# An opening stage written out channel by channel over three row ranges: a hybrid mLSTM / sliding-window-attention encoder

## The chip, the cores and the metric

One Trainium2 chip, one core. The metric is the device time of one execution in microseconds (us): the median of the runs, 1853.66 for the kernel before.

## The reference

Two sequences pass through the same two-layer trunk: a prompt of 256 rows and a sample of 512 rows, 1024 channels wide. Each layer computes six modulation vectors from a condition vector, mixes along the sequence (layer 0: an mLSTM with gates; layer 1: attention in a window), and applies a convolutional feed-forward network. What the change touches is the beginning of layer 0:

```python
mod = jax.nn.silu(c) @ adaln_w[l] + adaln_b[l]
sh1, sc1, g1, sh2, sc2, g2 = [t[:, None, :] for t in jnp.split(mod, 6, axis=-1)]
h = rmsnorm(x, norm_g[l, 0]) * (1 + sc1) + sh1
...
proj = h @ w_in          # q, k, v, o and the gates
```

`rmsnorm` multiplies each row by the inverse root of its mean square, and then each channel by a gain. So h is x times a *factor* of the row, times a *gain* of the channel (from `sc1` and the norm's weights), plus a *shift* of the channel (`sh1`).

## The kernel before, in words

All rows lie side by side as 768 columns: columns 0 to 255 are the prompt, 256 to 767 the sample. Channels are on the 128 partitions, in KC = 8 chunks ("channels" below means such a chunk). Work on columns goes over three ranges of 256: `RANGES = ((256, 512, 0), (512, 768, 0), PROMPT)`: two of the sample, then the prompt.

Each product is made of three: activations and weights are split into a rounded high part and the rest (`hh`, `hl`, tiles `zh`, `zl`; `whi`, `wlo`), and a matmul of them is high by high, high by low and low by high. The split of a weights tile of 128x1024 is a copy on ScalarE (`fp_copy_split`, L259) and a subtraction on VectorE (L260). Three `whi` and three `wlo` buffers exist, five `raw` buffers for loads, and eight `nt` buffers for temporaries. Matmuls issue from the helper `mm` (L253).

The opening, in `first` (L1510) and the beginning of `mlstm` (L633):

- `adaln(0, 0)` (L388) multiplies the condition by 16 tiles of 512 KB of `adaln_w` on TensorE as they land; its end (L418 to L439) evicts the result to `sb`, transposes it (L422), and makes `mod` (shift) and `gain`.
- `Norm` (L89) squares the eight channels of a range on ScalarE (L110), adds some squares on GpSimd (L114), sums the rest over partitions on TensorE against `inv` (L145), takes the power -0.5 on GpSimd (L152) and spreads the factor over a PSUM bank `pr` by a matmul. `scaled` (L556) multiplies x by it in place. This is done for the first two ranges while the tiles of `adaln_w` land; x of the second range and the gate weights `wg` are loaded between those tiles.
- `modulate` (L561) then applies gain and shift to the eight channels of both ranges (L565) and splits them.
- For the prompt, the norm sums all eight squares on TensorE, and `modulated` (L540) applies factor, gain and shift together (L548, L550, L551).
- `window` (L310) goes over the three ranges and, in each, over three weights tiles: the gates' and the two halves of q's for head 0, 24 matmuls each. The gates' bank is evicted by L646 and L647, q's by L262 and L263.

Behind it `mlstm` computes the gates' running sums and maxima on VectorE (L670 to L680), k's projection with `gemmT` (L292) into four `ps` banks, and v's with `gemmN` (L331), which needs those banks evicted (L259, L260). Among all this stand steps of `adaln_v` (L484, products L503 and L505 on VectorE), which makes layer 1's modulation from 48 tiles that go through the `raw` buffers, and of `adaln_g` on TensorE.

What sets the order: each engine runs its instructions in the order of the program. A scheduler chooses that order when the program is built, save where `manual_schedule` fixes the order of the named engines' instructions to that of the code; other instructions may still be put between them. All loads issue from SyncE, in order, and a load whose buffer isn't free holds those behind it.

## Time and profile before

| | us |
|---|---|
| runs: median (lowest to highest) | 1853.66 (1852.61 to 1855.81) |
| the profiled execution, first to last instruction | 1851.5 |
| TensorE busy | 1799.6 |
| VectorE busy | 1394.5 |
| ScalarE busy | 897.3 |
| GpSimd busy | 475.3 |
| mean granted clock of TensorE | 0.989 |

A line of the timeline gives start and duration in us, engine, line of the kernel, operation, what it writes and reads, the shape, a count, and in brackets how long the engine had been idle and who ended that. PE is TensorE, PEld its weight loads, DVE is VectorE, ACT ScalarE, POOL GpSimd, SPq the queue of SyncE. A line with a count above one merges instructions. The granted clock is 1.00 at full speed. The opening lies in the first 71 us.

### The profile page before, as it was taken

To read this page: it belongs to the slowest core of one execution; us is meant where nothing else is said; L and a number is where in the kernel's file an instruction comes from. 1 tells how busy PE (TensorE), PEld (TensorE's weight loads), DVE (VectorE), ACT (ScalarE), POOL (GpSimd) and SP (SyncE) were. 2 spreads that over 40 slices of the span, in tenths; PEclk is the share of its full clock that TensorE was granted. 3 is DMA by queue.
4 is the path that set the end of the run, shared out by engine and by line. 5 is a ranking of instruction groups with operands and counts; after the bars stand their busy time and mean duration, and the time that the engine had idled before them with its cause. 6 is when DMAs were issued, how large, how long until landed. Compare 5 with 4: busy or idle time off the path is not lost.

```text
span 1851.5 us, 29083 instructions
## 1 busy us (share of the span) xinstructions
PE 1799.6 (97%) x11290; PEld 1660.0 (90%) x11290; DVE 1394.5 (75%) x2292; ACT 897.3 (48%) x1815; POOL 475.3 (26%) x386
## 2 busy tenths in 40 slices
PE   6999999999999999999999999999999999999997
PEld 3987887888998999999999898889989999999997
DVE  4755676886689777777877858876898777777876
ACT  4444443443456444444444546765564444444443
POOL 1001001021024333333331313330134333333322
PEclk7999999999999999999999999999999999999999
DMA  8343556546312222222222321123122222222212
GB/s 329 117 147 132 174 190 223 168 139 201 106 46 80 69 69 69 68 69 69 68 69 83 104 82 49 52 94 121 51 92 69 69 69 69 69 69 69 69 35 69
DMA packets 64246, 184.49 MB, mean 100 GB/s; under 512 B 6167, under 2 KB 23831, under 8 KB 64108
## 3 DMA queue, kind: packets, MB, share of 16 engines
q1 hardware_dynamic: 64108, 182.63, 30.1%
q8 instruction: 89, 1.46, 0.3%
q14 instruction: 49, 0.40, 0.1%
HBM read 176.17 MB, written 6.43 MB: 99 GB/s over the span
## 4 chain that ended last, share of the span: by engine, by line
PE 86%; DVE 6%; DMA 3%; ACT 2%; issue 1%; POOL 1%; SPq 0%; POOLq 0%; ACTq 0%; DVEq 0%
PE ps L253 27%; PE pa L253 25%; PE ps L1163 10%; PE ps L1166 10%; PE ps L1164 10%; PE pa L1002 1%; DMA raw<-in_adaln_w_dram 1%; DVE wlo L260 1%; DMA raw<-in_w_dram 1%; DVE slab L589 1%; DMA slab<-in_adaln_w_dram 1%; PE pa L1166 0%; PE pa L1164 0%; PE pa L1163 0%; DMA slab<-mrows 0%
## 5 line engine op out<-in xcount | busy, mean ns | idle before, releaser
L259 ACT CAST whi<-raw 128x1024 fp32r<-128x1024 f32 x237 | 248.0, 1048 | 344.8 <-PE pa L253 162.0
L260 DVE TENSOR_TENSOR wlo<-raw,whi 128x1024 fp32r<-128x1024 f32 x237 | 322.3, 1361 | 113.7 <-ACT whi L259 111.7
L253 PE MATMUL pa<-slab,whi 128*128 128x256 f32 (+1 forms) x1472 | 346.5, 331 | 3.2 <-DVE slab L589 3.2
L253 PEld LDWEIGHTS pa<-slab,whi 128*128 128x128 f32 x1472 | 252.7, 188 | 27.5 <-DVE slab L589 4.6
L589 DVE SCALAR_TENSOR_TENSOR slab<-pa,mod,slab 128x256 f32<-128x256 f32 (+1 forms) x368 | 211.4, 593 | 69.6 <-PE pa L253 69.3
L253 PE MATMUL pa<-slab,wlo 128*128 128x256 f32 (+1 forms) x736 | 233.8, 330 | 0.0
L253 PE MATMUL ps<-zh,whi 128*128 128x256 f32 (+1 forms) x560 | 188.9, 338 | 2.3 <-ACT whi L259 1.7
L253 PE MATMUL ps<-zh,wlo 128*128 128x256 f32 (+1 forms) x560 | 184.1, 330 | 2.1 <-DVE wlo L260 2.1
L253 PE MATMUL ps<-zl,whi 128*128 128x256 f32 (+1 forms) x560 | 185.0, 332 | 0.0
L1163 PE MATMUL ps<-zh,whi 128*128 128x384 f32 x504 | 172.2, 342 | 3.7 <-ACT nt L1234 1.9
L1164 PE MATMUL ps<-zl,whi 128*128 128x384 f32 x504 | 169.9, 337 | 0.8 <-DVE zl L1120 0.8
L1166 PE MATMUL ps<-zh,wlo 128*128 128x384 f32 x504 | 168.9, 335 | 0.0
L253 PEld LDWEIGHTS pa<-slab,wlo 128*128 128x128 f32 x736 | 138.5, 188 | 13.1 <-DVE wlo L260 0.4
L1199 POOL TENSOR_TENSOR raw<-raw,raw 128x512 f32<-128x512 f32 x40 | 52.0, 1301 | 330.5 <-DVE wlo L260 246.1
L253 PE MATMUL ps<-slab,whi 128*128 128x384 f32 x512 | 132.2, 339 | 2.2 <-ACT sg L841 1.3
L1396 POOL TENSOR_TENSOR slab<-slab 128x772 f32<-128x772 f32 x44 | 86.5, 1967 | 171.5 <-DVE slab L1384 159.6
L1383 DVE SCALAR_TENSOR_TENSOR slab<-slab,cstt,slab 128x771 f32<-128x771 f32 x88 | 105.4, 1199 | 26.6 <-ACT slab L1381 26.4
L253 PEld LDWEIGHTS ps<-zh,whi 128*128 128x128 f32 x560 | 107.4, 192 | 15.9 <-issue 4.4
L505 DVE SCALAR_TENSOR_TENSOR ada<-raw,silc,ada 128x1024 f32<-128x1024 f32 x84 | 109.0, 1335 | 14.3 <-DMA raw<-in_adaln_w_dram 14.0
L253 PEld LDWEIGHTS ps<-zh,wlo 128*128 128x128 f32 x560 | 107.2, 192 | 12.4 <-DVE wlo L260 3.1
L253 PEld LDWEIGHTS ps<-zl,whi 128*128 128x128 f32 x560 | 107.2, 192 | 11.9 <-issue 3.4
L1196 POOL TENSOR_TENSOR raw<-raw 128x512 f32<-128x512 f32 x40 | 61.0, 1525 | 199.2 <-DMA raw<-in_w_dram 171.0
(294 smaller groups left out, 4303.0 us busy)
## 6 DMA issues: line engine op xcount, KB each, us to landing
raw<-in_w_dram SPq DMA_DIRECT2D x208, 512.0 KB, 3.7
raw<-in_adaln_w_dram SPq DMA_DIRECT2D x84, 512.0 KB, 4.6
slab<-in_x_dram SPq DMA_DIRECT2D x12, 512.0 KB, 7.1
slab<-in_adaln_w_dram SPq DMA_DIRECT2D x12, 512.0 KB, 10.3
slab<-mrows SPq DMA_DIRECT2D x8, 384.0 KB, 5.5
xs<-slab SPq DMA_DIRECT2D x6, 512.0 KB, 3.7
bt<-brow SPq DMA_DIRECT2D x16, 192.0 KB, 3.0
slab<-xs SPq DMA_DIRECT2D x6, 512.0 KB, 6.6
```

Source lines behind the costliest of these rows:

```text
L253: self.nc.tensor.matmul(out, lhsT, rhs, start=start, stop=stop)
L259: nc.scalar.copy(hi, src)
L260: return nc.vector.tensor_tensor(lo, src, hi.bitcast(F32), ALU.subtract)
L505: stt(acc[:, s], row, w, acc[:, s], ALU.mult, ALU.add)
L589: self.nc.vector.scalar_tensor_tensor(x, o, self.mod[l][:, gc + c, q : q + 1], x, ALU.mult, ALU.add)
L1163: mm(o, wh[:, k], hi[k], start=start and k == 0, stop=False, skip_group_check=True)
L1164: mm(o, wh[:, k], lo[k], start=False, stop=False, skip_group_check=True)
L1166: mm(o, wl[:, k], hi[k], start=False, stop=k == 3, skip_group_check=True)
L1196: tt(q[2], q[2], q[3], ALU.add)
L1199: tt(q[0], q[2], q[0], ALU.subtract)
L1383: stt(y[:, 1:], u[:, :-1], w(0), y[:, 1:], ALU.mult, ALU.add)
L1396: nc.gpsimd.tensor_tensor(y, y, yrow[:, j], ALU.mult)
```

## The change

`first` now runs `adaln` through, and issues all other loads of the opening behind it: `wg`, the second range of x, the two halves of q's weights, the prompt's x, `kct`. The second range's norm and scaling, the split of the gate weights, and `modulate` leave it. A new method `opening` takes the place of `window` and of what prepared it. It fixes the order on TensorE, ScalarE and VectorE for the first two ranges, and on TensorE and VectorE for the prompt:

- eight matmuls of `ones` by `ones`;
- the first range: gain and shift, high part, low part, one channel after the other, with matmuls of the high weights of the gates and the first half of q between; then the second half of q, then the three low weights. The squares of the second range stand between, all added on GpSimd;
- `stream` for the second range and the prompt: each channel gets factor, gain and shift in one product, and the matmuls of all three weights tiles follow at once. The squares of the prompt stand in the second range's stream, added on GpSimd too.

In the built order, `wg` stands in SyncE's queue behind both x ranges and `kct`; the eight constant matmuls stand between the two pairs of `adaln`'s transposes; three pairs of `adaln_v`'s products (L503 and L505 of before) stand on VectorE within the second range's stream and ahead of the prompt's; behind the opening, ScalarE evicts all three banks of the prompt before and between the next weights copies.

```diff
-    def mlstm(self, pool, gw, xt):
+    def mlstm(self, pool, raws, xt):
...
-        ws = [(gw, gates)] + [(w, keep(qt0, 0, c)) for c, w in self.halves(U_MIN)]
-        self.load_x(io["x"], RANGES[2:], xt)
-        nc.sync.dma_start(self.kct[:, P:], io["kc"][:, P : 3 * P])
-        norm = Norm(self, xt, PROMPT, self.modulated(0, 0), KC)
-        for c in range(KC):
-            norm.square(c)
-        self.start(PROMPT, norm.stages())
-        self.window(ws)
+        self.opening(xt, raws, (gates, keep(qt0, 0, 0), keep(qt0, 0, 1)))
...
+    def opening(self, xt, raws, sinks):
...
+        low = lambda i: tt(lo[i], raws[i], hi[i].bitcast(F32), ALU.subtract)
+        high = lambda i: nc.scalar.copy(hi[i], raws[i])
...
+        norms = {rng: Norm(self, xt, rng, keep_factor, 0) for rng in RANGES[1:]}
...
+        with self.tc.manual_schedule(engines={eng.PE, eng.Activation, eng.DVE}):
...
+            for _ in range(8):
+                self.mm(bank[0, 0][:, :P], self.ones, self.ones, True, True)
...
+            high(0)
+            for c in range(KC):
+                nc.vector.tensor_scalar(x(c), x(c), gain(c, q), shift(c, q), ALU.mult, ALU.add)
+                nc.scalar.copy(h(c), x(c))
+                if c == 1:
+                    high(1)
+                if c > 3:
+                    norms[r1].square(c - 4)
+                mm(r0, 0, 0, 0, c)
+                if c:
+                    lower(c - 1)
+                    mm(r0, 0, 0, 1, c - 1)
+                if c > 1:
+                    mm(r0, 1, 0, 0, c - 2)
+                    mm(r0, 1, 0, 1, c - 2)
+            lower(KC - 1)
+            high(2)
+            for c in range(4, KC):
+                norms[r1].square(c)
...
+            low(0)
+            for c in range(KC):
+                mm(r0, 2, 0, 0, c)
+                mm(r0, 2, 0, 1, c)
+            low(1)
+            for c in range(KC):
+                mm(r0, 0, 1, 0, c, c == KC - 1)
+            step(r1)
+            low(2)
...
+            def stream(rng, between):
...
+                for c in range(KC):
+                    t = self.tmp([P, n])
+                    stt(t, xt[c // 4][:, c % 4, c0:c1], gain(c, q), got[rng], ALU.mult, ALU.mult)
+                    nc.scalar.activation(self.hh[:, c, c0:c1], t, AF.Identity, bias=shift(c, q))
+                    for i in range(3):
+                        mm(rng, i, 0, 0, c)
+                        mm(rng, i, 1, 0, c)
+                    if made:
+                        later()
+                    made.append((c, t))
+                    if c in between:
+                        between[c]()
+                later()
...
+            stream(r1, {**{c: squares(c) for c in range(4)}, 5: lambda: step(r2), 7: lambda: step(r2)})
+        for i in range(3):
+            sinks[i](0, bank[i, 0])
+        with self.tc.manual_schedule(engines={eng.PE, eng.DVE}):
+            for i in range(3):
+                bank[i, 1] = self.pa()
+            stream(r2, {})
+        for i in range(3):
+            sinks[i](1, bank[i, 1][:, :256])
...
-        steps(4)
+        for _ in ada:
+            pass
+        raws = [self.raw(self.io["wg"]), self.load(U_MIN, 0)]
         self.load_x(x, RANGES[1:2], xt)
-        steps(2)
-        Norm(self, xt, RANGES[1], self.scaled).run()
-        self.graw = self.raw(self.io["wg"])
-        steps(2)
-        gates = self.split(self.graw)
-        for rng in RANGES[:2]:
-            self.modulate(xt, rng, 0, 0)
+        raws.append(self.load(U_MIN, 1))
+        self.load_x(x, RANGES[2:], xt)
+        self.nc.sync.dma_start(self.kct[:, P:], self.io["kc"][:, P : 3 * P])
```

51 lines of the change are left out of this document (49 added, 2 removed).

## The prediction

> **What bounds the kernel now.** I read the page first, then the stretches of 5 us, then the timeline of the first 90 us, since the diff ends there.
>
> ```profile
> span 1851.5 us, 29083 instructions
> ...
> PE 1799.6 (97%) x11290; PEld 1660.0 (90%) x11290; DVE 1394.5 (75%) x2292; ACT 897.3 (48%) x1815; POOL 475.3 (26%) x386
> ...
> PE 86%; DVE 6%; DMA 3%; ACT 2%; issue 1%; POOL 1%; SPq 0%; POOLq 0%; ACTq 0%; DVEq 0%
> ```
>
> TensorE is busy for 97% and is 86% of the chain that ends last. From the value projection on, the order of instructions on all engines stays the same but for a few neighbouring pairs, so the end moves by as much as the start of that projection moves. The median (1853.66) is 2.2 above the span; I add the shift to the median.
>
> ```profile
> 30.00:35.00 5.00, 4.44 (x26) 1.81 (x22) 3.16 (x9) 0.19 (x1) 0.00 (x0) 0.66 1.07 385
> 35.00:40.00 5.00, 4.76 (x24) 4.04 (x24) 4.29 (x16) 4.84 (x17) 0.00 (x0) 0.68 1.03 411
> 40.00:45.00 5.00, 5.00 (x24) 5.00 (x25) 5.00 (x14) 4.71 (x12) 0.00 (x0) 0.50 0.22 87
> ...
> 50.00:55.00 5.00, 5.00 (x44) 5.00 (x43) 3.66 (x9) 3.15 (x8) 0.00 (x0) 1.00 0.11 43
> ```
>
> Columns: PE, PEld, DVE, ACT and POOL busy (count), granted clock, DMA share, GB/s. DMA is full until about 40; the clock is 0.50 at 40 to 45 and 1.00 by 50, where TensorE never stops.
>
> ```profile
> 27.68 1.04 ACT L259 CAST whi<-raw 128x1024 fp32r<-128x1024 f32 x1 [5.02 <-DMA raw<-in_wg_dram]
> ...
> 36.13 5.26 DVE L565 TENSOR_SCALAR slab<-slab,gain,mod 128x256 f32<-128x256 f32 x16
> 37.67 5.28 PE L253 MATMUL pa<-inv,nt 128*128 128x2 f32 x24
> 42.81 0.56 PE L253 MATMUL ps<-zh,whi 128*128 128x256 f32 x1
> 44.45 0.41 PE L253 MATMUL ps<-zh,whi 128*128 128x256 f32 x1
> 44.67 0.41 PE L253 MATMUL ps<-zl,whi 128*128 128x256 f32 x1
> ...
> 70.98 0.40 PE L253 MATMUL ps<-zh,whi 128*128 128x512 f32 x1
> 74.09 0.95 DVE L670 TENSOR_TENSOR slab<-slab 36x768 f32<-36x768 f32 x1 [2.59 <-ACT slab L668]
> 88.27 0.39 PE L253 MATMUL ps<-whi,zh 128*128 128x256 f32 x1 [0.46 <-DVE slab L260]
> ```
>
> The opening's 216 matmuls run without a gap from 42.8 to 71.0: 0.215 us apart at half clock (two rows), about 0.12 at full (44 in 5.00). Then 16.6 us of key projection, a wait of only 0.46 for VectorE, and the value projection at **88.27**. Before 42.8 stand the modulation (36.13) and 24 mean sums (5.28).
>
> **What goes.** The 24 sums of the prompt (5.28) become two on TensorE after additions on GpSimd, and the second range's 12 sums and its eight scalings in place go too; those ran between modulation loads, where TensorE and VectorE waited for DMA anyway, so only the 5.28 counts, and it is contained in the earlier first matmul below. The 216 matmuls themselves stay.
>
> **Start of the new opening.** The gate weights move behind everything:
>
> ```profile
> 17.25 0.33 SPq L268 DMA_DIRECT2D raw<-in_wg_dram  x1
> 18.58 4.30 SPq L402 DMA_DIRECT2D slab<-in_adaln_w_dram  x4
> 23.84 1.66 SPq L379 DMA_DIRECT2D slab<-in_x_dram  x2
> 26.39 3.20 SPq L659 DMA_DIRECT2D kct<-in_kc_dram  x1
> ...
> slab<-in_x_dram SPq DMA_DIRECT2D x12, 512.0 KB, 7.1
> slab<-in_adaln_w_dram SPq DMA_DIRECT2D x12, 512.0 KB, 10.3
> ...
> kct<-in_kc_dram SPq DMA_DIRECT2D x1, 128.0 KB, 10.5
> ```
>
> In the new order the four modulation loads, the two x loads and kct that followed the gate weights go ahead of them: 6 x 512 + 128 KB = 3.28 MB, at 385 to 411 GB/s some 8.0 us. Arrival 27.7 + 8.0 = 35.7; q's two halves follow at 37.0 and 38.3. Modulation loads, freed of 1.57 MB ahead of them, end 3.8 us earlier, so the gain stands at some 32.3, which helps nothing: ScalarE's first copy in the new order waits for the gate weights. 35.7 + 1.04 + one copy of 0.33 (1.63/5, below): first matmul **37.1**, 5.7 sooner than 42.8.
>
> ```profile
> 30.23 1.22 PE L253 MATMUL pa<-kct,nr 128*128 128x128 f32 x4
> ```
>
> The eight constant matmuls stand between two pairs of transposes that the modulation needs. At 0.3 each (this row, clock 0.50) they take 2.4: 32.3 becomes 34.7, still under 35.7, so they cost nothing; were the weights early, 2.4. I count no gain: they end some 3 us before the first real matmul. The Trainium skill, "TensorE: Matmul & The Clock Gate", Part 1, says that the clock is released after a busy window of about 3.4 us and taken back after an idle one; by that rule too the eight are lost, and the sum stays.
>
> **First range.** Rows for the channel work and the sums:
>
> ```profile
> 40.91 1.63 ACT L259 CAST zh<-slab 128x256 fp32r<-128x256 f32 x5
> 46.52 1.22 DVE L260 TENSOR_TENSOR wlo<-raw,whi 128x1024 fp32r<-128x1024 f32 x1
> ...
> 20.86 3.93 POOL L114 TENSOR_TENSOR nt<-nt,nt 128x256 f32<-128x256 f32 x5 [5.56 <-ACT nt L110]
> 28.72 0.71 POOL L152 TENSOR_TENSOR nr<-nr,mhalf 128x2 f32<-128x2 f32 x1 [3.93 <-DVE nr L151]
> 46.36 3.29 POOL L152 TENSOR_TENSOR nr<-nr,mhalf 128x2 f32<-128x2 f32 x1 [16.93 <-DVE nr L151]
> ```
>
> 72 matmuls: 24 at half clock 5.2, 48 at full 5.8, waits of 0.8 (ScalarE's second weights copy) and 0.8 (mean sums and factor): 37.1 + 12.6 = **49.7**. Beside it GpSimd adds seven squares (3.93/5 = 0.79 each), the second square at 41, the sum at 46.6; with the power (0.71) the factor is there by 48.7. Nearly hidden. GpSimd's price is open: 0.71 and 3.29 are the same instruction, the longer beside VectorE's 1.22 us subtractions. Bounds for an addition: 0.73 to 1.4 (half of what that factor would make); I take 0.79, the nearest row: an addition of the same shape. At the lower end nothing is won, since TensorE's own work lasts as long.
>
> The Trainium skill, "SBUF — State Buffer", Who interferes with whom, says that a VectorE instruction with two SBUF inputs and a GpSimd one that reads SBUF exclude each other, the later blocked. The 3.29 row agrees, the 20.86 row can't tell; it is the rival below.
>
> **Second range and prompt.** On VectorE the new order puts products of the next layer's modulation *between* the channels: L503 after two channels, L505 after six, L505 ahead of the prompt.
>
> ```profile
> 51.34 3.22 DVE L548 SCALAR_TENSOR_TENSOR nt<-slab,gain,pa 128x256 f32<-128x256 f32 x8 [2.25 <-issue]
> 54.48 1.41 DVE L503 TENSOR_SCALAR ada<-raw,silc 128x1024 f32<-128x1024 f32 x2
> ...
> 55.91 0.33 SPq L268 DMA_DIRECT2D raw<-in_adaln_w_dram  x1
> 59.83 2.48 DVE L505 SCALAR_TENSOR_TENSOR ada<-raw,silc,ada 128x1024 f32<-128x1024 f32 x2 [0.78 <-DMA raw<-in_adaln_w_dram]
> ...
> raw<-in_adaln_w_dram SPq DMA_DIRECT2D x84, 512.0 KB, 4.6
> ...
> 56.78 0.68 ACT L646 ACTIVATE slab<-ps,cstt 36x512 f32<-36x512 f32 x1 [1.62 <-PE ps L253]
> 59.66 0.60 ACT L262 ACTIVATE slab<-ps 128x512 fp32r<-128x512 f32 x1 [1.50 <-PE ps L253]
> ```
>
> Each product's load goes into the buffer that the last one freed and lands 3.9 later (55.91 to 59.83). The first buffer is freed by the third weights subtraction, at 48.6 in the new order: load 52.5, L503 till 53.8, load 57.7, L505 till 60.2, load 64.1, L505 till **66.5**. Columns of the raw row: size, median us to landing. The landing is open: 3.9 here, 4.6 in the median of 84, down to about 3.2; each 0.5 moves the window's end by about as much. Before, VectorE had nothing urgent queued behind those waits; now the channels stand there, and behind them ScalarE's copies and TensorE. TensorE's second range, 72 x 0.12 = 8.6 from 49.7, stops 1.8 and 3.0 there and 0.5 at the first channels, with 0.4 of sums and factor: **64.1**. The prompt's first product follows at 66.5 (0.40, L548's mean), then ScalarE; without L505 it would still wait for four evictions of the sample (2 x 0.68 + 2 x 0.60 = 2.6) that the order puts ahead: 67.5, then 8.6 and one wait of 0.8: **76.9**. With TensorE idle for 3 us twice, I add one spell of half clock. Its price is an estimate: 16 to 18 matmuls, as many as ran 0.215 apart between 42.8 and the full clock, each 0.1 longer: 1.7. None to two such spells are possible. Window ends **78.6** against 71.0: **+7.6**.
>
> **Tail.** Before, the gates' matmuls ended 5.7 us ahead of the window, so their evictions and the next weights ran beneath q's matmuls. Now all three banks end together, all three weight buffers with them.
>
> ```profile
> 66.30 0.47 ACT L646 ACTIVATE slab<-pa,cstt 36x256 f32<-36x256 f32 x1
> 67.28 0.85 ACT L666 ACTIVATE slab<-slab 36x768 f32<-36x768 f32 x1
> ...
> 69.66 1.28 ACT L667 ACT_TABLE_LOAD   x1
> 73.12 0.94 ACT L668 ACTIVATE slab<-slab,ones 36x768 f32<-36x768 f32 x1
> ```
>
> ScalarE after the window: two gate evictions 0.94, two q evictions 0.7, three weight copies 3.1, then 0.85 + 1.28 + 0.85 + 1.28 + 0.94: 9.9 until VectorE's first gate step, which stood 3.1 after the window's end (74.09). From it to the value projection 14.2, less 1.2 and 0.4 for a weights subtraction and an eviction that now stand earlier: 12.6. So 22.5 after the window instead of 17.3: **+5.2**. TensorE's 3 us without weights lie inside this.
>
> Sum: 7.6 + 5.2 = 12.8; 1853.66 + 12.8 = **1866.5**.
>
> **Rivals.** (1) The products' loads are there in time: without these waits the same sum ends the window at 73.1, no spell of half clock: 2.1 + 5.2, **1861.0**. For it: loads may start sooner; against: the 0.78 wait of 59.83. (2) GpSimd is shut out: additions of 1.4 delay the first factor by 4 and the window to 81.5, plus 1.7 and 5.2: 17.4, **1871.1**. It decides once an addition exceeds about 0.8. For: 3.29, and the skill's rule on the shared port, which would give this case; against: 3.93 for five. (3) The stream runs gapless: 37.1 + 5.2 + 192 x 0.12 + 1.0 = 66.3, the tail's 5.2 eats the 4.7 won: **1854.2**. (4) Faster, on the other side: as (3), and the value projection waits for matmuls, not for the gates: 66.3 + 17.3 against 88.27, -4.7, **1849.0**. It holds if the gate chain after the window is under 17.3 instead of 22.5; its ScalarE rows speak against it.
>
> **How the numbers follow.** Forecast 50%, (1) 20%, (2) 20%, (3) 6%, (4) 4%. The range takes in (1) less 3 for a shorter landing and (2) plus 3 for a second spell of half clock: 1858 to 1874, leaving out (3) and (4). Within 0.2% (3.7 us, about what a measurement tells from no change) lies (3); faster 0.05, same 0.07, slower 0.88.
>
> **What would show it.** The gate weights' copy at 35.7; first matmul at 37; VectorE's L505 rows with DMA waits inside the second range; TensorE idle ahead of the prompt and again after the window; the value projection near 101. Wrong if that row stands under 90.

## The result, and the profile after

| | before | after |
|---|---|---|
| median of the runs (lowest to highest), us | 1854.74 (1852.61 to 1856.36) | 1877.18 (1875.62 to 1879.06) |
| profiled execution, us | 1851.5 | 1876.6 |
| mean granted clock of TensorE | 0.989 | 0.988 |

The ratio is 1.0123, 95% interval 1.0107 to 1.0139: slower by some 22 us, where +12.8 was forecast. The same kernel measured once more, as a yardstick for the experiments (c0_again below), gave 1.0116.

First the page of the changed kernel: the span, busy times, and the chain that ended last by engine.

```profile
span 1876.6 us, 29048 instructions
...
PE 1804.7 (96%) x11270; PEld 1663.8 (89%) x11270; DVE 1395.6 (74%) x2284; ACT 901.1 (48%) x1815; POOL 488.0 (26%) x395
...
PE 80%; DVE 8%; issue 4%; DMA 3%; ACT 3%; POOL 1%; SPq 0%; POOLq 0%; DVEq 0%; ACTq 0%
```

TensorE was busy for 5 us more; VectorE's share of the chain rose from 6% to 8% and TensorE's fell from 86% to 80%. 6% of the span are over 100 us, far more than the 22 lost, so these shares say little about the opening; the rows below do. Next the stretches of 5 us of the changed kernel (columns as above):

```profile
35.00:40.00 5.00, 1.10 (x3) 0.79 (x3) 1.41 (x4) 2.84 (x6) 0.00 (x0) 0.55 0.97 386
40.00:45.00 5.00, 4.87 (x23) 4.87 (x24) 4.75 (x11) 4.15 (x12) 2.49 (x3) 0.50 0.06 25
...
50.00:55.00 5.00, 4.00 (x23) 3.80 (x24) 2.18 (x4) 0.49 (x2) 1.67 (x2) 0.76 0.54 187
...
65.00:70.00 5.00, 3.54 (x17) 3.54 (x18) 3.54 (x8) 1.02 (x2) 0.71 (x1) 0.66 0.31 105
70.00:75.00 5.00, 2.26 (x15) 2.05 (x14) 4.33 (x9) 3.25 (x6) 0.00 (x0) 0.81 0.33 107
75.00:80.00 5.00, 5.00 (x26) 5.00 (x25) 4.82 (x12) 3.06 (x6) 0.00 (x0) 0.51 0.00 0
```

Where TensorE did 44 matmuls in 5 us at full clock before, it now does 23, 17 and 15, with idle time and a clock below 1.00 again and again. The timeline of the changed kernel, in the order of the forecast's steps, says what it waited for:

```profile
37.16 1.05 ACT L849 CAST whi<-raw 128x1024 fp32r<-128x1024 f32 x1 [6.05 <-DMA raw<-in_wg_dram]
38.56 0.89 PE L253 MATMUL ps<-zh,whi 128*128 128x256 f32 x2 [5.37 <-ACT zh L887]
42.35 2.70 POOL L114 TENSOR_TENSOR nt<-nt,nt 128x256 f32<-128x256 f32 x3 [25.55 <-ACT nt L110]
45.42 4.61 POOL L114 TENSOR_TENSOR nt<-nt,nt 128x256 f32<-128x256 f32 x4 [0.36 <-ACT nt L110]
50.09 0.61 PE L253 MATMUL pa<-inv,nt 128*128 128x2 f32 x4 [0.87 <-POOL nt L114]
50.97 1.64 POOL L152 TENSOR_TENSOR nr<-nr,mhalf 128x2 f32<-128x2 f32 x1 [0.94 <-DVE nr L151]
52.66 1.22 PE L253 MATMUL pa<-kct,nr 128*128 128x128 f32 x4 [0.91 <-POOL nr L152]
53.53 2.06 PE L253 MATMUL ps<-zh,wlo 128*128 128x256 f32 x8
53.99 0.87 DVE L935 SCALAR_TENSOR_TENSOR nt<-slab,gain,pa 128x256 f32<-128x256 f32 x2 [1.95 <-PE pa L253]
56.65 2.37 DVE L503 TENSOR_SCALAR ada<-raw,silc 128x1024 f32<-128x1024 f32 x2
60.01 0.39 PE L253 MATMUL ps<-zh,whi 128*128 128x256 f32 x1 [1.29 <-ACT zh L936]
62.92 2.48 DVE L505 SCALAR_TENSOR_TENSOR ada<-raw,silc,ada 128x1024 f32<-128x1024 f32 x2 [1.27 <-DMA raw<-in_adaln_w_dram]
66.46 0.58 PE L253 MATMUL ps<-zh,whi 128*128 128x256 f32 x1 [2.61 <-ACT zh L936]
68.99 2.48 DVE L505 SCALAR_TENSOR_TENSOR ada<-raw,silc,ada 128x1024 f32<-128x1024 f32 x2 [1.28 <-DMA raw<-in_adaln_w_dram]
70.88 0.68 ACT L646 ACTIVATE slab<-ps,cstt 36x512 f32<-36x512 f32 x1 [3.69 <-PE ps L253]
73.83 0.58 PE L253 MATMUL pa<-zh,whi 128*128 128x256 f32 x1 [2.74 <-ACT zh L936]
84.50 0.88 PE L253 MATMUL pa<-zl,whi 128*128 128x256 f32 x6
94.84 0.95 DVE L663 TENSOR_TENSOR slab<-slab 36x768 f32<-36x768 f32 x1 [3.50 <-ACT slab L661]
107.60 0.58 PE L253 MATMUL ps<-whi,zh 128*128 128x256 f32 x1 [2.60 <-DVE slab L260]
```

The last low weights of the first range end at 53.53 + 2.06 = 55.6. The window ends at 84.50 + 0.88 = 85.4 (71.1 before, which the forecast took as 71.0; 78.6 forecast), the value projection starts at 107.6 (88.27 before, 101.1 forecast). A row further on that stands in both kernels, the first eviction of layer 0's other modulation, gives the shift with which the opening leaves:

```profile
173.93 0.24 DVE L529 TENSOR_TENSOR mod<-ps,cstt 128x8 f32<-128x8 f32 x2 [0.54 <-PE ps L522]
```

```profile
194.31 0.24 DVE L529 TENSOR_TENSOR mod<-ps,cstt 128x8 f32<-128x8 f32 x2 [0.54 <-PE ps L522]
```

The first is the kernel before, the second the one after: +20.4 of the +25.1 between the two spans. In c0_again the same row stood at 192.67: +18.7. I call this row the *marker*. Behind it the changed kernel is later by another 4.7 (5.2 in c0_again). The edited kernels below lie between -1.6 and +4.1 there, x12 at +7.2, and the spans of the runs of the kernel before alone reach from 1847.9 to 1856.5. I don't explain what comes behind the marker.

### The profile page after: what moved, and what is told of

The parts are those of the page before. It is cut to its first block, busy times and chain, and to the rows that moved or that the text cites. A ratio compares the mean times of both kernels' runs of the same rounds, so it can differ in the third digit from the quotient of the medians.

```text
span 1876.6 us, 29048 instructions
## 1 busy us (share of the span) xinstructions
PE 1804.7 (96%) x11270; PEld 1663.8 (89%) x11270; DVE 1395.6 (74%) x2284; ACT 901.1 (48%) x1815; POOL 488.0 (26%) x395
## 4 chain that ended last, share of the span: by engine, by line
PE 80%; DVE 8%; issue 4%; DMA 3%; ACT 3%; POOL 1%; SPq 0%; POOLq 0%; DVEq 0%; ACTq 0%
PE pa L253 24%; PE ps L253 23%; PE ps L1274 10%; PE ps L1277 10%; PE ps L1275 10%; DVE ada L505 1%; PE pa L1113 1%; DMA raw<-in_adaln_w_dram 1%; DVE wlo L260 1%; DVE slab L589 1%; DMA slab<-in_adaln_w_dram 1%; PE pa L1274 0%; PE pa L1277 0%; PE pa L1275 0%; DMA raw<-in_wg_dram 0%
## 5 line engine op out<-in xcount | busy, mean ns | idle before, releaser
L260 DVE TENSOR_TENSOR wlo<-raw,whi 128x1024 fp32r<-128x1024 f32 x234 | 314.7, 1346 | 116.0 <-ACT whi L259 114.1
L253 PE MATMUL ps<-zh,whi 128*128 128x256 f32 (+1 forms) x560 | 190.1, 342 | 14.4 <-ACT zh L887 5.8
L505 DVE SCALAR_TENSOR_TENSOR ada<-raw,silc,ada 128x1024 f32<-128x1024 f32 x84 | 111.7, 1368 | 12.6 <-DMA raw<-in_adaln_w_dram 12.5
L253 PEld LDWEIGHTS ps<-zh,wlo 128*128 128x128 f32 x560 | 106.3, 193 | 11.8 <-DVE wlo L260 2.6
```

The source lines that it names most:

```text
L253: self.nc.tensor.matmul(out, lhsT, rhs, start=start, stop=stop)
L260: return nc.vector.tensor_tensor(lo, src, hi.bitcast(F32), ALU.subtract)
L505: stt(acc[:, s], row, w, acc[:, s], ALU.mult, ALU.add)
```

## The experiments

Window end is the last prompt product's start plus duration, v the value projection's first matmul, marker the shift of the row above; all in us of one profile. The difference is that of the medians of one batch.

| kernel | ratio (95%) | difference | window end | v | marker |
|---|---|---|---|---|---|
| before | | | 71.1 | 88.3 | |
| after | 1.0123 (1.0107 to 1.0139) | +22.4 | 85.4 | 107.6 | +20.4 |
| c0_again | 1.0116 (1.0101 to 1.0131) | +20.2 | 83.5 | 105.7 | +18.7 |
| e1_fill_behind | 1.0095 (1.0080 to 1.0110) | +17.3 | 80.5 | 106.3 | +15.4 |
| e3_weights_early | 1.0098 (1.0081 to 1.0115) | +16.3 | 79.9 | 101.8 | +12.7 |
| e2b_sums_dve | 1.0173 (1.0153 to 1.0194) | +33.6 | 94.9 | 116.8 | +31.0 |
| e2_sums_pe | 1.0171 (1.0142 to 1.0199) | +29.9 | 94.1 | 116.4 | +29.6 |
| e4_gates_first | 1.0101 (1.0085 to 1.0118) | +17.6 | 84.8 | 103.9 | +18.2 |
| e6_no_ones | 1.0103 (1.0085 to 1.0121) | +18.8 | 82.6 | 104.8 | +18.0 |
| w1_warm | 1.0097 (1.0081 to 1.0114) | +18.5 | 83.5 | 105.4 | +20.3 |
| x1 | 1.0081 (1.0065 to 1.0097) | +13.9 | 77.2 | 101.8 | +15.9 |
| b1_prompt_sums | 1.0019 (1.0010 to 1.0028) | +3.2 | 75.5 | 92.8 | +4.5 |
| e7_norm1_ahead | 1.0086 (1.0073 to 1.0100) | +16.0 | 80.6 | 102.5 | +14.2 |
| e8_norms_ahead | 1.0063 (1.0049 to 1.0076) | +11.5 | 77.0 | 98.9 | +12.2 |
| x6 | 1.0039 (1.0025 to 1.0052) | +8.3 | 77.9 | 97.0 | +8.9 |
| x8 | 1.0022 (1.0013 to 1.0031) | +4.7 | 73.0 | 94.0 | +6.4 |
| x9 | 1.0019 (1.0010 to 1.0028) | +4.0 | 74.0 | 95.1 | +5.9 |
| x10 | 1.0030 (1.0019 to 1.0041) | +4.4 | 72.3 | 93.6 | +4.0 |
| x11 | 1.0038 (1.0023 to 1.0053) | +5.9 | 72.9 | 94.2 | +6.9 |
| x12 | 1.0074 (1.0060 to 1.0087) | +14.0 | 72.2 | 89.8 | +5.7 |

The intervals of several single edits touch c0_again's. There the profile's rows decide what is read, and only where they and the medians agree.

### One part at a time

**c0_again**: the changed kernel, unedited.

> The changed kernel as it is, beside the runs of the others, as their yardstick. Expected under every theory: 1.012 of the kernel before (1877 us), first matmul at 38.6 us, window end at 85.2, value projection at 107.6, each within about 0.5.

The time came as expected. The first matmul (37.91), the window's end and v came 0.7, 1.7 and 1.9 earlier than expected. Differences of about 2 us between two profiles are therefore not read as effects below.

**e1_fill_behind**

```diff
+                    self.hold = stt(self.hl[:, c, c0:c1], ...)   # last of the opening
 def step(self, gen, n=1):
-    for _ in range(n):
-        next(gen, None)
+    with self.tc.issue_after(self.hold.ins):
+        for _ in range(n):
+            next(gen, None)
```

> The products of the next layer's modulation (L503, L505) leave the streams of channels and stand on VectorE behind the opening. Theory W (the waits for the products' loads are what stretches the two streams): in the changed kernel the two L505 groups and one L503 group took 2.4 + 2.5 + 2.5 us of VectorE and 2.5 us of DMA waits inside the window; the window should end 4 to 6 us earlier (near 80) and the time fall by 4 to 6, as far as the products find room in the tail where VectorE waits for ScalarE (5.5 us). Rival G (GpSimd's additions and VectorE shut each other out, and the stream is late from the first range on): the window moves by no more than 1 to 2 us, since the prompt then waits for its sums. Rival D (the loss is made behind the opening, by products that come late): window earlier, time unchanged.

The window ended at 80.5, near the 80 of theory W. That is 4.9 earlier than in the profile from which the expectation started, but 3.0 earlier than in c0_again, and the median fell by 3. With the products gone, another wait stood in the second range's stream: VectorE waited 3.0 us at 63 for the prompt's two sum matmuls, which stand in TensorE's queue behind the channels (L151), and the prompt's first matmul still came at 70.1. The products took their time behind the window instead, between the gates' steps: v didn't come sooner. So W is right in part, and so is D.

**e2b_sums_dve** and **e2_sums_pe**

```diff
-norms = {rng: Norm(self, xt, rng, keep_factor, 0) for rng in RANGES[1:]}
+norms = {rng: Norm(self, xt, rng, keep_factor, 0, adds=nc.vector) for rng in RANGES[1:]}          # e2b_sums_dve
+norms = {rng: Norm(self, xt, rng, keep_factor, KC if rng == RANGES[1] else 0, adds=nc.vector) ...} # e2
```

> The squares of the second range and the prompt are added up on VectorE and no longer on GpSimd. Rival G: GpSimd's additions took 0.9 to 1.15 us each beside VectorE and the pow 1.64, and VectorE's own instructions beside them were longer (3.43 for two where 2.26 stood before); taking them off GpSimd brings the second factor some 2 to 4 us sooner and the window's end with it. Theory W: VectorE gets 14 more additions of about 0.35 us (4.9 us in all) into a queue that already sets the pace, so the window ends at the same place or up to 3 us later; only the first range gains at most 1.

> The second range's squares are summed over channels by TensorE itself (one small matmul per square and half, as in the kernel before) and the prompt's are added on VectorE; GpSimd adds nothing. With the sums on VectorE in both ranges the time rose by some 10 us over the changed kernel, because each addition waits in VectorE's queue for ScalarE's square and the channels stand behind it. Theory Q (whatever waits for ScalarE in VectorE's queue ahead of the channels sets the pace): the first factor comes about 2 us sooner than in the changed kernel (the rows show a wait of 1.8 for the last addition and 0.9 for the power), the prompt's eight additions still cost about half of those 10 us, so the time is 2 to 5 us over the changed kernel. Rival G (GpSimd's exclusion by VectorE is the main loss): at or below the changed kernel, by up to 4 us.

All theories were far off: 10 to 13 us slower than the changed kernel. VectorE of e2b, first the subtractions of two low weights in the first range, then the second range:

```profile
48.97 2.35 DVE L848 TENSOR_TENSOR wlo<-raw,whi 128x1024 fp32r<-128x1024 f32 x2
...
57.88 0.43 DVE L114 TENSOR_TENSOR nt<-nt,nt 128x256 f32<-128x256 f32 x1 [1.26 <-ACT nt L110]
...
62.56 0.42 DVE L114 TENSOR_TENSOR nt<-nt,nt 128x256 f32<-128x256 f32 x1 [0.48 <-ACT nt L110]
64.35 1.28 DVE L505 SCALAR_TENSOR_TENSOR ada<-raw,silc,ada 128x1024 f32<-128x1024 f32 x1 [1.36 <-DMA raw<-in_adaln_w_dram]
```

An addition costs 0.42, half of GpSimd's, but it waits in VectorE's queue for ScalarE's square, and the next channel stands behind it. e2 kept seven of the fourteen on VectorE, those between the second range's channels, and put 32 sum matmuls (3.63 us) on TensorE for the rest. It lost nearly as much. In both, the second factor was used 2 us later than in the changed kernel (56.1 against 53.99), and some 7 us more of the window were lost behind that, where both have the same seven additions between the channels. That the place and not the number of additions costs is argued from this. GpSimd, slow as it is, was the better place.

**e3_weights_early**

```diff
-        for _ in ada:
-            pass
-        raws = [self.raw(self.io["wg"]), self.load(U_MIN, 0)]
-        self.load_x(x, RANGES[1:2], xt)
-        raws.append(self.load(U_MIN, 1))
-        self.load_x(x, RANGES[2:], xt)
+        for _ in range(6):
+            next(ada)
+        raws = [self.raw(self.io["wg"])]
+        for _ in ada:
+            pass
+        raws += [self.load(U_MIN, 0), self.load(U_MIN, 1)]
+        self.load_x(x, RANGES[1:], xt)          # issued behind the weights
```

> The gate weights' load is issued between the modulation loads and q's two halves ahead of the x tiles of the second range and the prompt; all else as in the changed kernel. Late-weights theory: ScalarE's first copy waited for the gate weights until 37.2 us while the gain stood at 33.7; with the weights in time the gain ends last, the first matmul starts near 35.7 instead of 38.6, and the value projection and the time come 2.5 to 3 us sooner. Theory W: the streams wait for loads of the products and for the second range's sums further down, so of these 3 us under 1.5 reach the window's end. The modulation loads behind the gate weights come 1.3 us later, which could take half of the gain away.

First matmul at 35.84, window 3.6 and v 3.9 earlier than in c0_again, median 4 less: the late-weights theory, and 1 more than its 2.5 to 3.

**e4_gates_first** and **e6_no_ones**

```diff
-                    for i in range(3):
+                    for i in range(n_in):        # 3, and 2 in the prompt's stream
...
+                for i in range(n_in, 3):         # behind all channels
+                    for c in range(KC):
+                        mm(rng, i, 0, 0, c)
+                        mm(rng, i, 1, 0, c)
+                        mm(rng, i, 0, 1, c, c == KC - 1)
```

```diff
-            for _ in range(8):
-                self.mm(bank[0, 0][:, :P], self.ones, self.ones, True, True)
```

> In the prompt's stream the gates and q's first half are taken, and q's second half follows when all channels are there; otherwise the changed kernel. Tail theory: all three banks and all three weight buffers end together, so gate evictions, the next weights and the gates' chain start only at the window's end (22.4 us from there to the value projection, 17.3 before). With the gates' bank ready 24 matmuls (2.9 us at full clock) ahead of the end, ScalarE's gate evictions and the first weights copy go beneath them: tail 2 to 3 us shorter, time 2 to 3 us under the changed kernel. Rival (the tail is ScalarE's queue in its own order, and its evictions wait for the last bank anyway): no change, within 1 us.

> The changed kernel without the eight constant matmuls ahead of the first range. They take 1.95 us between two pairs of transposes that the modulation needs. My theory: the first real matmul waits for ScalarE's copy of the gate weights, which land 3 us after the gain, so the time is the same within 1.5 us. Rival (they wake the clock): without them the first range runs more matmuls at half clock, some 0.1 us each, up to 2 us longer. Other rival (they delay the modulation on the path): up to 2 us shorter.

The tail of e4, from window end to v, is 103.9 - 84.8 = 19.1 instead of 22.2, as expected; but the window ended 1.3 later, and the intervals of both kernels overlap that of c0_again. The eight constants cost and bring nothing that can be measured.

**w1_warm**

```diff
-            for _ in range(8):
-                self.mm(bank[0, 0][:, :P], self.ones, self.ones, True, True)
+            with self.tc.issue_after(self.turned.ins):        # adaln's last transpose
+                for _ in range(20):
+                    self.mm(bank[0, 0][:, :P], self.ones, self.ones, True, True)
```

> The changed kernel with 20 constant matmuls in place of 8, all behind the modulation's transposes, so that TensorE is busy (about 4.9 us at the 0.24 us of a constant matmul in the changed kernel) where it waited 5.4 to 6 us for the gate weights. Clock theory: in the changed kernel the clock fell to a half about 2.5 us into that wait and the first range's matmuls then ran 0.215 us apart for 5 to 7 us; kept busy, they run 0.12 apart from the start, the first range's half-clock time shrinks by 2 to 5 us and the second factor, behind it on TensorE, comes 1 to 2 us sooner: time 1 to 2 us less. Rival: the first range then waits for its channels on VectorE and ScalarE (0.66 us a channel for three to four matmuls) and for GpSimd's sums, so the time is the same within 1 us. Other rival: the constants end late and delay the first real matmul, up to 1 us more.

Three stretches of w1_warm, then TensorE's constants and its sum of the second range:

```profile
35.00:40.00 5.00, 2.65 (x16) 1.94 (x16) 2.82 (x9) 3.86 (x8) 0.00 (x0) 1.00 0.95 379
40.00:45.00 5.00, 4.62 (x32) 3.97 (x33) 4.86 (x8) 4.31 (x12) 3.67 (x4) 1.00 0.01 3
...
50.00:55.00 5.00, 4.08 (x20) 3.88 (x20) 2.73 (x6) 2.03 (x6) 1.82 (x3) 0.54 0.35 113
```

```profile
30.80 4.63 PE L253 MATMUL ps<-ones 128*128 128x128 f32 x40
48.55 0.61 PE L253 MATMUL pa<-inv,nt 128*128 128x2 f32 x4 [1.83 <-POOL nt L114]
```

The clock held at 1.00 where it was 0.55 and 0.50 (0.63 and 0.69 in c0_again), and the window ended at 83.5, where c0_again's does. The faster matmuls wait 1.83 for GpSimd's last addition, and behind that wait the clock fell to 0.54 (0.76 in the changed kernel, 0.67 in c0_again). So the constants moved the half clock to behind the wait, and the time stayed within what can be told apart: the rival of the expectation.

### Several together

**x1**: the edits of e1, e3, e4 and e6, and

```diff
-        for i in range(3):
-            sinks[i](0, bank[i, 0])
-        with self.tc.manual_schedule(engines={eng.PE, eng.DVE}):
+        with self.tc.manual_schedule(engines={eng.PE, eng.Activation, eng.DVE}):
...
-            stream(r2, {})
+            stream(r2, {2 + 2 * i: (lambda i=i: sinks[i](0, bank[i, 0])) for i in range(3)}, 2)
```

> Five corrections together on the changed kernel: the modulation's products behind the opening, the gate weights and q's halves loaded ahead of the x tiles, gates and q's first half alone in the prompt's stream, the sample's evictions between the prompt's channels on ScalarE, no constant matmuls. If the losses add up (products 3, weights 4, banks 2 to 3, evictions up to 3, constants 0 to 2): 12 to 15 us under the changed kernel, 1858 to 1861, still 4 to 8 over the kernel before. If they hide each other (the sums on GpSimd then end last): 5 to 8 under.

6 under the changed kernel, the second case of the expectation: the four single edits took 2.9, 3.9, 2.6 and 1.4 off the median, 10.8 in all, and together with the moved evictions only 6.3. The window ended 6.3 earlier than c0_again's, but the products that had left it stood in the gates' steps, and the tail grew to 24.5.

**b1_prompt_sums**: an edit of the kernel *before*.

```diff
-        norm = Norm(self, xt, PROMPT, self.modulated(0, 0), KC)
+        norm = Norm(self, xt, PROMPT, self.modulated(0, 0), 0)
```

> The kernel before with one part of the change alone: the prompt's eight squares are added on GpSimd and summed by two small matmuls, where TensorE had 24 passes (5.28 us) ahead of its first product. My theory: these sums stood on the path (37.67 to 42.8, the gain ready at 36.13), so the first matmul starts near 38 instead of 42.8; some of it is lost again as more of the window runs at half clock or waits for the first channels: 2 to 4 us faster than before. Rival (the window is held by VectorE's channels and by weights anyway): within 1 us of before. Rival G: the additions take turns with VectorE's subtractions, the prompt's factor comes late, 1 to 3 us slower.

Slower by 3.2 us (1.9 to 5.2 by the interval): in size that is rival G. VectorE's products of gain and shift, then TensorE of b1_prompt_sums:

```profile
37.23 8.15 DVE L565 TENSOR_SCALAR slab<-slab,gain,mod 128x256 f32<-128x256 f32 x16
```

```profile
38.61 0.38 PE L253 MATMUL ps<-zh,whi 128*128 128x256 f32 x1 [2.37 <-ACT zh L259]
43.11 0.58 PE L253 MATMUL ps<-zh,whi 128*128 128x256 f32 x1 [4.12 <-ACT whi L259]
45.77 0.58 PE L253 MATMUL ps<-zl,whi 128*128 128x256 f32 x1 [2.07 <-DVE zl L260]
```

With the sums gone TensorE waits for ScalarE's weights copy and then for VectorE's low part. The 24 sums had stood largely beside that wait, not in front of it. The loss stands in VectorE's row: the 16 products took 8.15 where they took 5.26 before, while GpSimd's seven additions ran from 36.44 to 42.97, each 0.73 and so not lengthened. VectorE's low parts behind them began at 45.30 instead of 41.30, and the window's end came 4.4 and v 4.5 later. From 45.77 to the window's end TensorE had no wait, so it was not the prompt's factor that came late, as rival G has it, but VectorE's work beside the additions.

**e7_norm1_ahead** and **e8_norms_ahead**: x of the second range, its sums and its scaling ahead of the gate weights, as before; in e8 the prompt's squares and sums also beside the first range.

```diff
+        self.load_x(x, RANGES[1:2], xt)                      # behind four tiles of adaln
+        Norm(self, xt, RANGES[1], self.scaled).run()         # behind six, then wg
-                    norms[r1].square(c - 4)
+                    norms[r2].square(c - 4)                  # e8 alone
-            stream(r1, {**{c: squares(c) for c in range(4)}, 5: ..., 7: ...})
+            stream(r1, {})                                   # e8 alone
```

> The changed kernel with the second sample range put back ahead of the gate weights: its x tiles, sums and scaling stand between the modulation loads as in the kernel before, and the gate weights' load where it was; the opening is still written channel by channel, the prompt's squares still in the second range's stream. Theory: the second range's place and the late weights make most of the loss. Then the first matmul starts near 37 to 38, no wait for the second factor (1.8 + 0.9 + the subtraction behind it), the second range ends near 62, and the time is 8 to 11 us under the changed kernel. Rival (the products and the prompt's sums behind them end last): 3 to 5 under, as with the weights alone.

> As the kernel with the second range put back, and the prompt's squares and sums made beside the first range, where the second range's stood. Theory G for the second stream: GpSimd's and ScalarE's squares beside the second range's channels cost it 1 to 2 us and the prompt waits for its factor, so 2 to 4 us less than with the second range put back alone. Rival (the products' loads end last there): no difference.

e7 is no better than the early weights alone: the rival. VectorE and the prompt's first matmul in e7, then the same matmul in e8:

```profile
59.30 2.48 DVE L505 SCALAR_TENSOR_TENSOR ada<-raw,silc,ada 128x1024 f32<-128x1024 f32 x2 [2.58 <-DMA raw<-in_adaln_w_dram]
65.37 2.48 DVE L505 SCALAR_TENSOR_TENSOR ada<-raw,silc,ada 128x1024 f32<-128x1024 f32 x2 [1.54 <-DMA raw<-in_adaln_w_dram]
```

```profile
70.19 0.58 PE L253 MATMUL pa<-zh,whi 128*128 128x256 f32 x1 [2.74 <-ACT zh L933]
```

```profile
63.17 0.28 PE L253 MATMUL pa<-zh,whi 128*128 128x256 f32 x1
```

With the second factor no longer late, the products' loads are: 2.58 and 1.54 of DMA waits where the changed kernel had 1.27 and 1.28. Its first matmul came at 38.38, no sooner than c0_again's, so what e7 gained it gained behind the start and not, as e3 did, by the start. In e8 the prompt's steps left the second range's stream too; the products fell otherwise there (the scheduler's choice; waits of 0.95 and 0.71). The prompt's first products stood at 63.17, among the sample's last ones, the bulk of them followed from 68.23, and the window ended 3.6 earlier. With e1 this shows two covers over the same time: without the products (e1) or without the second range's factor (e7), the other wait still holds the prompt's start at 70.

**x6**: the edits of e8 and e6, the gates alone in the prompt's stream (`n_in` 1), and the products behind the gates' scans. **x8**: x6 with the sample's evictions behind the prompt's channels, and ScalarE's order fixed there too. **x9**: x8 and constants in two waits.

```diff
+            self.hold = scan(M[32:36, b][:, ::-1], ...)       # x6: step() issues behind it, as in e1
```

```diff
+        with self.tc.issue_after(self.last.ins):              # x8: the prompt's last high part
+            for i in range(3):
+                sinks[i](1, bank[i, 1][:, :256])
+                sinks[i](0, bank[i, 0])
```

```diff
+                for _ in range(5):                            # x9: behind adaln's transposes
+                    self.mm(bank[0, 0][:, :P], self.ones, self.ones, True, True)
...
+                if c == 2:
+                    for _ in range(7):
+                        self.mm(bank[2, 0][:, :P], self.ones, self.ones, True, True)
```

> The previous one, and the gates alone in the prompt's stream with q's two halves behind them, the products of the modulation behind the gates' scans, no constant matmuls. If the three losses named so far (second range's place, products in the queue, gates' bank ending with q) are all that the change lost, the window ends near 68 and the value projection starts near 84 to 88: 0 to 5 us faster than before. If the streams' own pace (VectorE and ScalarE about 0.8 to 0.9 us a channel, half-clock spells) holds the window, it ends near 72 to 74 and the time is 2 to 6 us over before.

> The kernel with the second range ahead, the gates alone in the prompt's stream, the products behind the scans and no constants, and now with the sample's three bank evictions behind all the prompt's channels on ScalarE and VectorE. There the prompt's channels waited behind the sample's gate eviction (TensorE short of work by about 3 us between 64.5 and 70, then a half-clock spell of 3.4 us, 1.7 lost). Theory: the prompt's gates follow the second range without a gap, the window ends 3 to 5 us sooner; the gates' chain then starts behind two evictions of 0.68 more: time 2 to 4 us less than the kernel without this edit, that is 3 to 6 over before. Rival: the chain of the gates, not the window, sets the value projection: no gain, or 1 us more.

> As the previous one, and five constant matmuls behind the transposes and seven behind the first channels, where TensorE waited 1.35 and 1.98 us, to hold the clock. If the clock at the head is worth what the half-clock rows say (5 to 8 us at 0.215 instead of 0.12 apart, 2 to 3 us lost), time 1 to 3 us less than without them and 1 to 4 over before. If the first range is paced by its channels, weights and sums, the same within 1 us.

x6 came out worse than its second case: the scheduler put the sample's evictions between the prompt's channels, and those waited for the second range's end. x8 shows the price of that place (in the changed kernel the row at 70.88 and TensorE's 2.74 us): window 4.9 earlier, median 3.6 less, though the intervals overlap a little. x9 measures the same as x8.

**x10**: x9 with the prompt's sums and factor in the second range's stream. **x11**: x10 with the gates' last exponential held back.

```diff
-            step(r2)                                          # x10: both, of the first range
...
-            stream(r1, {})
+            stream(r1, {2: lambda: step(r2), 5: lambda: step(r2)})
```

```diff
+                with self.tc.issue_after(self.late.ins):      # x11: the gate matrix's exponential
                     nc.vector.tensor_tensor(F, F, M, ALU.add)
                     nc.scalar.activation(F, F, AF.Exp, scale=-1.0)
```

> As the kernel with the constants in the waits, but the prompt's two small sum matmuls and its factor stand in the second range's stream (behind its third and sixth channel) instead of inside the first range. Theory G (GpSimd's slow additions cost the time because TensorE stands in order behind them): the waits of 1.8 and 0.9 us go, and with them most of a half-clock spell (1.7): 3 to 4 us less, within 1 us of the kernel before. Rival (the first range is paced by the low weights' subtractions and channels): under 1 us less.

> As the previous one, and the gates' exponential of F with its addition is held back until the first exponentials of the gate matrix, so that ScalarE's key evictions no longer stand behind the gates' scans. Tail theory: TensorE's wait of 2.3 us ahead of the value projection goes: 1.5 to 2.5 us less than the previous one, 0 to 3 us faster than before. Rival: the wait moves to the scores, which need the gates' columns anyway: no change.

The wait of 1.8 went and the clock stood at 1.00 in every stretch from 35 to 90; the window came to 72.3, within 1.2 of before; the time didn't fall, so for the time the rival holds. In x11 it didn't fall either, and TensorE still waited 2.60 ahead of the value projection: the tail theory failed. What is left lies behind the window. VectorE of x10 around the key evictions:

```profile
87.12 1.42 DVE L504 TENSOR_SCALAR ada<-raw,silc 128x1024 f32<-128x1024 f32 x2
88.45 0.94 DVE L773 TENSOR_TENSOR slab<-slab 36x768 f32<-36x768 f32 x1
89.31 1.21 DVE L260 TENSOR_TENSOR wlo<-raw,whi 128x1024 fp32r<-128x1024 f32 x1
90.45 2.47 DVE L506 SCALAR_TENSOR_TENSOR ada<-raw,silc,ada 128x1024 f32<-128x1024 f32 x2
...
92.88 0.67 DVE L260 TENSOR_TENSOR slab<-ps,slab 128x512 fp32r<-128x512 f32 x1
```

The key's last matmul started at 88.65; the evictions that free its banks stand behind 3.9 us of products.

**x12**: x11, and the products behind the value projection's first evictions.

```diff
-                    self.fp_copy_split(v[:, 0, t, :256], v[:, 1, t, :256], o)
+                    self.hold = self.fp_copy_split(v[:, 0, t, :256], v[:, 1, t, :256], o)
```

> As the previous one with the exponential held back, and the products of the modulation held back until the value projection's first evictions, so that neither stands ahead of the key evictions. Theory: the 2.6 us in which TensorE waits for VectorE's key eviction ahead of the value projection, and some 2 us around it, go: 3 to 4.5 us less than the kernel with the prompt's factor moved, from 1 us slower to 2 us faster than before. Rival (the products' late reads hold weight buffers, so that the next weights or the gates' row transfers, queued behind their loads, come late): the gain is lost again behind the value projection, no change or slower.

The value projection came at 89.8, 1.5 behind before: with it the opening's loss was undone but for that. And the time was 14 us over before, the rival. What SyncE's queue waited for in x12 between 85 and 125 us (in all, times, longest), and what TensorE waited for between 88 and 480:

```profile
SPq L268 <- DVE ada L504: 10.4, 1, 10.4
...
SPq L268 <- DVE ada L506: 6.4, 1, 6.4
```

```profile
PE ps L253 <- DMA raw<-in_adaln_w_dram: 2.7, 2, 1.6
```

Before, that queue stood behind VectorE's products for 2.5 us in the same stretch (and for 27.9 behind TensorE, 5.9 in x12), and no wait of TensorE for these loads is among its largest seven. Held back, the products keep the `raw` buffers, and all loads queue behind them. The marker stood at +5.7, the span ended at +12.9; the waits above are part of it, and the rest I did not take apart. No kernel here beats the one before; x8 and x9 come nearest, 1.002.

## Why the prediction was wrong, step by step

**Right: slower, the waits that were named, the tail.** The copy that waits for the gate weights, the DMA waits ahead of L505, and TensorE idle ahead of the prompt and behind the window all stand in the trace. The tail came within 0.3: 107.6 - 85.4 = 22.2 after the window, 22.5 forecast. In e4, with the gates' bank ready earlier, it was 19.1.

**The step that failed: the price of GpSimd's sums in the first range.** The forecast took an addition at 0.79 and the power at 0.71, had the second factor "there by 48.7. Nearly hidden", and ended the range at "49.7". That is 7 x 0.79 + 0.71 = 6.2; measured were 2.70 + 4.61 + 1.64 = 8.95, and the same in c0_again (2.71 + 4.62 + 1.64). The two additions that ran beside VectorE's two-input subtractions of 128x1024 were the long ones (shortest, middle and longest in ns, first and last start in us), the other five took 0.72 to 1.00:

```profile
L114 POOL TENSOR_TENSOR nt<-nt,nt x2: 1315/1458/1602, 45.4 to 46.8; 128x256 f32<-128x256 f32 x2
```

So the factor wasn't hidden. TensorE waited 0.87 for the last addition (50.09) and 0.91 for the power (52.66), VectorE could use the factor at 53.99, and the range ended at 55.6, 5.9 late. Of these 5.9, 1.5 is the gate weights, whose copy started at 37.16 instead of 35.7. 1.8 is the two waits. 1.1 is the eight matmuls behind them, 2.06 instead of the 0.96 that eight take at full clock. The granted clock was 0.76 from 50 to 55, but that the waits brought it down is argued, not shown. The last 1.5 is spread over the range: 28 matmuls near half clock instead of 24, and the sums and the factor themselves. As an estimate, at the forecast's 0.79 the last addition would have been done at 42.35 + 0.36 + 5.53 = 48.2, ahead of TensorE, which came to it at 49.2.

The Trainium skill's rule on the shared port ("SBUF — State Buffer", Who interferes with whom), weighed in the prediction, was the truer guide: beside two-input subtractions the additions took 1.46 on average, and the pow beside one 1.64. So rival (2) came true in part: its 1.4 for two additions of seven, 1.04 for the mean of all, and together with the forecast's own waits, not in their place. (The rule that the prediction gives for 1.4, half of the factor 3.29 / 0.71 on 0.79, makes 1.8.) What this step is worth in the total is not shown: in x10 the first range no longer waited for GpSimd, and the time was that of x9.

**Second range and prompt: right in length, in part by luck.** From 55.6 to 70.9, where ScalarE's first eviction shows the second range's end, it took 15.3 instead of 14.4, and the prompt from there to 85.4 the 14.5 of the forecast (64.1 to 78.6). So the window's 6.8 beyond 78.6 are 5.9 + 0.9. The parts differ. TensorE's stops were 1.29 and 2.61 (60.01 and 66.46) instead of 1.8 and 3.0, and the first had another cause: L503 waited for no load, its two products took 2.37 beside GpSimd's additions, 1.41 before and in e2b. Half clock made up for it: 0.66 from 65 to 70 and 0.51 from 75 to 80, where one spell was counted. Of these spells only the one at the head was tried (w1_warm).

**A term that was right by luck.** The forecast took the prompt's 24 sums as 5.28 on the path before 42.8. In the kernel before, TensorE had to wait in any case for ScalarE's second weights copy:

```profile
39.96 1.04 ACT L259 CAST whi<-raw 128x1024 fp32r<-128x1024 f32 x1
```

It ended at 41.0, so at most 1.8 of the 5.28 stood on the path, and in b1_prompt_sums taking the sums out brought nothing. It did no harm, since the new first matmul was worked out from the gate weights.

**The rest.** With window and tail, v is 6.5 behind its forecast, +19.3 against before. In c0_again it is +17.4. The medians say 22.4 and 20.2. These last 3 us come behind v, and their cause stays open.

**What the change lost, by the medians of the ladder.** From 20.2 (c0_again): late gate weights 4 (e3), by an earlier start. On another branch, the second range's place 4 (e7), without an earlier start; whether these two are the same 4 us no run tells. From e7 on, the prompt's steps out of the stream 4.5 (e8); products, gates' bank and constants 3 (x6); evictions ahead of the prompt 3.6 (x8). Some 4 to 5 are left (x8 to x10). The rows point to the products: in e1 and x10 they stand ahead of what the value projection needs, in x12 the loads stand behind them. That they are all of it is not shown. Before, the kernel had its products at 54, 60 and 66, where VectorE had nothing urgent queued behind.

## What to carry to other kernels

In a stage where several engines hand work on in order, waits lie on top of each other: mending one shows the next, and what single experiments gain can't be added up (10.8 alone, 6.3 together in x1). Price an addition on GpSimd from a row where VectorE is doing what it will be doing then. And background work that frees load buffers has a place to keep: moved forward it stands in the stream, moved back it starves the loads.

## What the runs showed of the hardware

VectorE and GpSimd slowed each other, both ways. The rows of the changed kernel, VectorE's two subtractions beside the first two of GpSimd's four additions above, and its third with only the pow:

```profile
44.39 3.43 DVE L848 TENSOR_TENSOR wlo<-raw,whi 128x1024 fp32r<-128x1024 f32 x2
50.81 1.23 DVE L848 TENSOR_TENSOR wlo<-raw,whi 128x1024 fp32r<-128x1024 f32 x1
```

1.72 each instead of 1.23, while the pow went from 0.71 to 1.64 and the third subtraction lost nothing. In e2b, with the additions off GpSimd, the same two subtractions took 2.35 together instead of 3.43. Products with a single tile as input lengthened too, L503 from 1.41 to 2.37 and in b1 L565 from 5.26 to 8.15, there with GpSimd's additions at their usual 0.73. The Trainium skill, "SBUF — State Buffer", Who interferes with whom, has it that a VectorE instruction with two SBUF inputs and a GpSimd one that reads SBUF exclude each other, and that issue order decides who blocks: the trace agrees, in that both engines were found longer, each beside the other.

In w1_warm 40 small constant matmuls in an idle wait (4.63 us) held the granted clock at 1.00, where the changed kernel's was 0.55 and c0_again's 0.63. The Trainium skill, "TensorE: Matmul & The Clock Gate", Part 1, tells of a clock released by a busy window and taken back by an idle one; the trace agrees. Here the held clock brought no time that could be measured: TensorE then waited 1.83 for GpSimd, and the clock fell to 0.54 behind that wait.
